# Start order, one moved statistic and new mixer delays in a two-layer decoder trunk on one Trainium2 core

## Chip, cores and metric

One Trainium2 chip, one core used. The metric is the device time of the program in microseconds; before the change the median of three runs is 1355.22 us (1355.17 to 1356.07).

## What is computed

Two layers over x of 256 tokens by 1024 features, float32. Each layer runs three sub-layers, each with a norm before and one after:

```
for i in range(DEPTH):                                   # 2 layers
    f = swiglu_ffn(rmsnorm(x, pre), w_in, w_out)         # 1024 -> 2*2816 -> 1024
    x = x + 0.5 * rmsnorm(f, post)
    p = rmsnorm(x, mpre) @ mix_w_in                      # q, k, v, z, beta, a, glu, gates
    y_a = gated_deltanet(...)                            # conv4+silu on q,k,v; chunked delta rule; norm; w_o
    y_b = conformer_conv(...)                            # a*sigmoid(g); 31-tap causal conv; layernorm; silu; w_o
    x = x + rmsnorm((g_a * y_a + g_b * y_b) @ mix_w_out, mpost)
    f = swiglu_ffn(rmsnorm(x, pre2), w_in2, w_out2)
    x = x + 0.5 * rmsnorm(f, post2)
```

## The kernel before

Tokens stand in two blocks of 128 (`tb` 0 and 1). All weights are streamed from HBM once, in pieces of 128 by 1024 (512 KB), some of 128 by 544. `Stream.load_one` issues a piece's transfer on SP's queue into `raw` (four buffers), ScalarE casts it into `whi` (the high part), and VectorE or GpSimd subtracts to get `wlo` (the low part). Activations are split in the same way into `xt` high and low. Every product is then three matmuls (`mm3`): high by high, high by low, low by high. In the profile such a matmul is `mm<-whi,xt` or `mm<-wlo,xt`.

A program order is written out for TensorE (`manual_schedule`). Products of a projection run in the order of the pieces, and after each pair of k tiles `lanes.tick()` is called. `Lanes` holds side jobs, generators that issue a few instructions at each step (transposes, convolutions, the delta rule, casts). A job's step comes due a number of ticks after the one before it, and that number stands in the table `DELAY`; `PLAN` gives the order of the mixer's column chunks and which jobs each one starts; `AFTER` and `LATE` say which jobs must be over, and by how many ticks, before one starts; the 31-tap convolution (`c0` to `c3`, accumulators `cacc`) and the inverse (`inv`, tile `iu`) have no due time and fill VectorE and GpSimd. In `Stream` a piece's cast and subtraction come due `lag` and `lag2` ticks after its load. ScalarE, VectorE and GpSimd then run in the order that the scheduler makes of all this, with the priorities in `CFG`; every engine executes its list in order.

The places that the prediction speaks of:

- **The start** (`start`, `half`, lines 470 to 525 of the kernel): seven matmuls on zeros (`idle`), then x is transposed in groups of four 128 by 128 tiles (`tr<-cst,x`; the identity `cst` and the scale `first_w` come on ScalarE's queue). ScalarE writes the four high parts `xt`, VectorE the four low parts. SP's first issues are: x of block 0 in two halves, the first weight piece, all of x of block 1, four more pieces. The first chunk of the first FFN takes its four pieces one after another, both token blocks for each. A job `first` does block 1's two transposed halves, then the two sums of squares (`jk`).
- **The end of each sub-layer** (`post`): for a token block, ScalarE squares and sums the two 512-column accumulators (`jk`), VectorE scales them into `fw`, adds up the sums (`ss`), GpSimd takes the power (`rpost`), VectorE adds to x. It runs twelve times; only the last one has no products beside it.
- **From FFN1 to the mixer** (`pre`, jobs `pre0` and `pre1`): the new x is normed into `xw`, transposed in halves, and split into `xt` while the last products of the FFN and the first of the mixer run.
- **The middle of the mixer**: VectorE does the short convolutions `c`, the decay products `at`, the 31-tap convolution and most `wlo`, each of them in its turn.

Of the kernel before, what the change touches and what calls it, by code (L numbers as in the profile page):

```python
# [9 lines left out]
F32 = mybir.dt.float32  # L10
# [5 lines left out]
P = 128  # L16
# [29 lines left out]
    "first": (1, 2), "ffn": (3, 5, 12), "pre0": (13, 7, 8, 4, 3, 3), "pre1": (15, 16, 0, 13, 8),  # L46
    "yt0": (10, 0, 10, 10, 26), "yt1": (10, 2, 0, 3, 3), "f_g0": (5, 0, 2, 1), "f_g1": (5, 1, 1, 1), "c0": (0, 0),
    "f_k1": (0, 1, 3, 1, 1, 3), "f_ka": (2, 0, 3), "decays": (12, 4, 2, 15, 4), "dts": (51, 3, 0, 0, 19, 19),
# [197 lines left out]
class Stream:  # L246
# [16 lines left out]
    def load_one(self, parts=1):  # L263
# [5 lines left out]
        nc.sync.dma_start(raw[:, :n], src)  # L269
# [54 lines left out]
def trunk(ctx: ExitStack, tc: tile.TileContext, x_in, wfirst, consts, feat, pch, tokp,  # L324
# [62 lines left out]
    for hf in range(2):  # L387
        nc.sync.dma_start(x[0][:, hf * 512:hf * 512 + 512], x_in[0:P, hf * 512:hf * 512 + 512])
        if hf == 0:
            nc.scalar.dma_start(cst[:, 0:P], consts[:, 0:P])  # L390
            nc.scalar.dma_start(first_w, wfirst)
# [87 lines left out]
    def start():  # L479
        r = [small(1, f"rstd{tb}") for tb in range(2)]  # L480
        xh = [halves(tb) for tb in range(2)]

        def half(tb, hf):
            tr = ps_tr()
            for k in range(4):
                T.transpose(tr[:, k, :], x[tb][:, (hf * 4 + k) * P:(hf * 4 + k + 1) * P], ident)
            t = xh[tb][hf]
            for k in range(4):
                S.activation(t[:, 0, k, :], tr[:, k, :], AF.Copy, scale=first_w[:, hf * 4 + k:hf * 4 + k + 1])
            for k in range(4):  # L490
# [971 lines left out]
```

## Time and profile before

| | us |
|---|---|
| median of three runs | 1355.22 |
| the profiled execution | 1356.38 |
| its span, from the first to the last instruction | 1354.4 |
| around the span | 1.98 |

The profile belongs to an execution of its own, 1.16 us above the median of the runs. TensorE is busy in 98% of the span, VectorE in 68%, ScalarE in 54%, GpSimd in 33%. With TensorE this full, read where it is *not* busy, or runs slowly, and follow what ended each of those times.

### The profile page before, as it was taken

The page shows a single profiled execution, that of the slowest core. Times are in us where ns is not written, and L with a number is a line of the kernel's source. Part 1 is how long each engine was busy: PE and PEld are TensorE (multiplying, and loading weights), DVE is VectorE, ACT ScalarE, POOL GpSimd, SP SyncE. Part 2 cuts the span into 40 slices and gives each one's busy share as a digit, 9 for nine tenths or more (in the row PEclk, how much of TensorE's full clock was granted, in tenths as well). Part 3 has the DMA queues.
Part 4 walks back from the last instruction along what each step waited for, and adds up shares of the span by engine and source line. Part 5 has one row for each costly group of instructions (what it writes and reads, how often), then busy time and mean ns, then how long its engine had stood idle before and what let it go on. Part 6 is the DMA issues. An engine that isn't in the chain of part 4 may idle for free.

```text
span 1354.4 us, 20203 instructions
## 1 busy us (share of the span) xinstructions
PE 1331.3 (98%) x7259; PEld 1132.3 (84%) x7259; DVE 926.9 (68%) x1593; ACT 730.8 (54%) x1172; POOL 446.4 (33%) x372
## 2 busy tenths in 40 slices
PE   9999999998999999999999999999989999999998
PEld 7888878997888888888888888799978878888886
DVE  6666456999966676765476654579999566766553
ACT  6554447666555545554455553577555564555541
POOL 0111025798834201111001110278986432011110
PEclk9999999999999999999999999999999999999999
DMA  7877745553634666876478775464545446477760
GB/s 273 284 259 248 232 164 192 185 191 114 196 125 147 212 229 207 281 253 218 148 230 278 263 236 186 143 233 172 172 143 166 151 139 233 157 258 254 257 225 33
DMA packets 114644, 273.76 MB, mean 202 GB/s; under 512 B 24656, under 2 KB 47728, under 8 KB 114544
## 3 DMA queue, kind: packets, MB, share of 16 engines
q1 hardware_dynamic: 114256, 272.40, 60.1%
q8 instruction: 57, 0.93, 0.3%
q14 instruction: 43, 0.35, 0.1%
q10 hardware_dynamic: 288, 0.07, 0.0%
HBM read 256.68 MB, written 15.75 MB: 201 GB/s over the span
## 4 chain that ended last, share of the span: by engine, by line
PE 81%; DVE 9%; POOL 3%; ACT 3%; issue 2%; DMA 1%; DVEq 0%; POOLq 0%; ACTq 0%
PE mm L143 75%; PE gd L143 4%; DVE cacc L123 3%; DVE c L123 3%; PE tr L149 2%; POOL wlo L123 2%; DVE wlo L123 2%; DMA raw<-mw 1%; ACT whi L170 1%; POOL rk L123 1%; DVE at L123 1%; ACT dt L170 1%; PE gd L149 0%; ACT sg L170 0%; ACT cf L170 0%
## 5 line engine op out<-in xcount | busy, mean ns | idle before, releaser
L143 PE MATMUL mm<-whi,xt 128*128 128x512 f32 (+1 forms) x2048 | 648.4, 392 | 4.8 <-ACT qT L170 2.3
L170 ACT CAST whi<-raw 128x1024 fp32r<-128x1024 f32 (+2 forms) x445 | 459.4, 1041 | 321.6 <-PE mm L143 201.4
L123 DVE TENSOR_TENSOR wlo<-raw,whi 128x1024 fp32r<-128x1024 f32 (+1 forms) x341 | 425.0, 1258 | 199.3 <-ACT whi L170 193.5
L143 PEld LDWEIGHTS mm<-whi,xt 128*128 128x128 f32 x2048 | 383.2, 188 | 85.2 <-DVE xt L123 4.9
L143 PE MATMUL mm<-wlo,xt 128*128 128x512 f32 (+1 forms) x1024 | 396.7, 387 | 0.5 <-DVE wlo L123 0.5
L123 POOL TENSOR_TENSOR wlo<-raw,whi 128x1024 fp32r<-128x1024 f32 (+1 forms) x104 | 247.4, 2394 | 142.5 <-ACT whi L170 138.1
L143 PEld LDWEIGHTS mm<-wlo,xt 128*128 128x128 f32 x1024 | 193.1, 189 | 37.2 <-DVE wlo L123 1.0
L143 PE MATMUL mm<-whi,act 128*128 128x512 f32 x704 | 218.3, 390 | 0.0
L123 POOL TENSOR_TENSOR act<-way,act 128x512 fp32r<-128x512 f32 x44 | 78.6, 1785 | 406.1 <-ACT act L170 396.4
L123 DVE SCALAR_TENSOR_TENSOR cacc<-hT,pc,cacc 128x254 f32<-128x254 f32 (+28 forms) x464 | 179.5, 470 | 0.2
L143 PE MATMUL mm<-xt,whi 128*128 128x256 f32 x960 | 175.0, 284 | 0.5 <-ACT qT L170 0.5
L143 PEld LDWEIGHTS mm<-whi,act 128*128 128x128 f32 x704 | 132.2, 188 | 27.5
L143 PEld LDWEIGHTS mm<-xt,whi 128*128 128x128 f32 x960 | 149.5, 192 | 1.2 <-ACT qT L170 0.8
L143 PE MATMUL mm<-wlo,act 128*128 128x512 f32 x352 | 137.0, 389 | 0.0
L143 PE MATMUL mm<-xt,wlo 128*128 128x256 f32 x480 | 135.8, 283 | 0.0
L143 PEld LDWEIGHTS mm<-xt,wlo 128*128 128x128 f32 x480 | 92.0, 192 | 0.0
L170 ACT ACTIVATE ag<-mm,rstd 128x256 f32<-128x256 f32 x88 | 41.8, 475 | 91.3 <-PE mm L143 75.2
L123 DVE SCALAR_TENSOR_TENSOR ag<-mm,rstd,ag 128x256 f32<-128x256 f32 x88 | 42.4, 481 | 54.0 <-ACT ag L170 53.8
L143 PEld LDWEIGHTS mm<-wlo,act 128*128 128x128 f32 x352 | 66.1, 188 | 13.5
L123 POOL TENSOR_TENSOR rpost<-ss,exp 128x1 f32<-128x1 f32 x12 | 6.5, 538 | 194.1 <-DVE ss L123 194.1
L123 DVE SCALAR_TENSOR_TENSOR fw<-mm,wbc 128x512 f32<-128x512 f32 x24 | 16.5, 687 | 46.4 <-ACT jk L170 46.4
L170 ACT ACTIVATE jk<-mm 128x512 f32<-128x512 f32 x24 | 14.4, 598 | 62.3 <-PE mm L143 62.3
(187 smaller groups left out, 1180.7 us busy)
## 6 DMA issues: line engine op xcount, KB each, us to landing
raw<-mw SPq DMA_DIRECT2D x168, 512.0 KB, 3.7
raw<-w1i SPq DMA_DIRECT2D x88, 512.0 KB, 4.7
raw<-w2i SPq DMA_DIRECT2D x88, 512.0 KB, 4.8
raw<-w1o SPq DMA_DIRECT2D x44, 512.0 KB, 4.3
raw<-w2o SPq DMA_DIRECT2D x44, 512.0 KB, 4.2
way<-way SPq DMA_DIRECT2D x176, 64.0 KB, 1.8
way<-way SPq DMA_DIRECT2D x44, 256.0 KB, 4.8
wbc<-feat SPq DMA_DIRECT2D x13, 512.0 KB, 4.5
```

Of the source, the lines that this page charges most:

```text
L123: r = op(out, *a, **k)
L143: r = self.eng.matmul(o, w, x, **k)
L149: r = self.eng.transpose(*a)
L170: r = op(*a, **k)
```

## The change

Five edits. (1) x and the first two pieces are loaded in parts and in the order of use, with the first transposes two at a time (`turn`), and each of the two first pieces is cast and subtracted in two halves, with the casts placed by hand. (2) In the first chunk (`lead`) pieces are taken two at a time for each token block. (3) In `post` the sum `ss` and the power are issued ahead of the second `fw`. (4) The tables `PLAN`, `DELAY`, `LATE`, `POOL` and some numbers of `CFG` are new. (5) The second part of `cst` and the first `wbc` are loaded later.

```diff
 PLAN = [
...
-    ("q0", ["f", "qt0"]), ("q1", ["f", "qt1", "qs", "cn"]), ("v0", ["f", "vt0"]), ("z0", ["s1", "s0"]),
+    ("q0", ["f", "qt0"]), ("q1", ["f", "qt1", "qs", "cn", "s1"]), ("v0", ["f", "vt0"]), ("z0", ["s0"]),
...
 DELAY = {
-    "first": (1, 2), "ffn": (3, 5, 12), "pre0": (13, 7, 8, 4, 3, 3), "pre1": (15, 16, 0, 13, 8),
+    "first": (1, 1, 4, 4, 3, 2, 2), "ffn": (20, 5, 36), "pre0": (13, 0, 8, 4, 0, 0),
+    "pre1": (15, 40, 10, 13, 8, 8, 8), "yt0": (10, 0, 10, 10, 26, 23, 26, 26), "yt1": (10, 0, 3, 3, 3, 3),
...
-LATE = {"inv": 20, "cn": 12, "sim0": 6, "sim1": 6, "merge": 7, "dts": 14}
+LATE = {"inv": 21, "cn": 15, "sim0": 6, "sim1": 7, "merge": 11, "dts": 10}
...
@@ load_one
-        nc.sync.dma_start(raw[:, :n], src)
+        for k in range(parts):
+            c = slice(k * n // parts, (k + 1) * n // parts)
+            r = nc.sync.dma_start(raw[:, c], src[:, c])
+            self.last = getattr(r, "ins", r)
...
+        if parts > 1:
+            yield
         for k in range(parts):
-            if k:
-                yield
             c = slice(k * n // parts, (k + 1) * n // parts)
             high(c)
+            if parts > 1:
+                yield
             low(c, self.gp if self.side[i] else self.vec)
+            if parts > 1:
+                yield
@@ start
+        def turn(tb, ks):
+            tr = ps_tr()
+            for i, k in enumerate(ks):
+                T.transpose(tr[:, i, :], x[tb][:, k * P:(k + 1) * P], ident)
...
         piece = st.load_one(2)
-        half(0, 0)
         next(piece)
-        nc.sync.dma_start(x[1], x_in[P:2 * P, :])
-        half(0, 1)
+        nc.sync.dma_start(x[0][:, 2 * P:4 * P], x_in[0:P, 2 * P:4 * P])
+        second = st.load_one(2)
+        next(second)
+        nc.sync.dma_start(x[1][:, 0:4 * P], x_in[P:2 * P, 0:4 * P])
+        nc.sync.dma_start(x[0][:, 4 * P:], x_in[0:P, 4 * P:])
+        pair = turn(0, (0, 1))
+        next(piece)
+        next(pair)
+        next(piece)
+        next(pair, None)
+        next(piece)
         next(piece, None)
 
         def steps():
+            for _ in turn(0, (2, 3)):
+                pass
+            for _ in second:
+                pass
+            yield
             half(1, 0)
+            st.load()
+            nc.sync.dma_start(x[1][:, 4 * P:], x_in[P:2 * P, 4 * P:])
+            yield
+            half(0, 1)
             st.load()
             yield
             half(1, 1)
@@ post
+        r = small(1, "rpost")
         for hf in range(2):
             cs = slice(hf * 512, hf * 512 + 512)
             S.activation(jk[:, cs], acc[hf], AF.Square, scale=D ** -0.5, accum_out=ss[:, hf:hf + 1])
+            if hf:
+                rms_scale(r, ss[:, 0:1], ss[:, 1:2])
             V.scalar_tensor_tensor(fw[:, cs], acc[hf], half, wbc[:, cs], op0=ALU.mult, op1=ALU.mult)
-        r = small(1, "rpost")
-        rms_scale(r, ss[:, 0:1], ss[:, 1:2])
@@ proj_in
-            for i in range(8 // chunks[c][1]):
+            b = 2 if lead and c == 0 else 1
+            for i in range(0, 8 // chunks[c][1], b):
                 for tb in range(c < first, 2):
-                    piece(c, tb, i, ps[tb], st.peek(0))
-                st.done()
+                    for j in range(b):
+                        piece(c, tb, i + j, ps[tb], st.peek(j))
+                for j in range(b):
+                    st.done()
```

Three places show what the engines' lists became.

**ScalarE at the start.** Its casts of weights (`whi`) and the high parts of x (`xt`), before:

```order
L170 ACTIVATE xt<-tr,first_w 128x128 x4
L170 CAST whi<-raw 128x512
L170 ACTIVATE xt<-tr,first_w 128x128 x4
L170 CAST whi<-raw 128x512
L170 ACTIVATE xt<-tr,first_w 128x128 x4
L170 CAST whi<-raw 128x1024
L170 ACTIVATE xt<-tr,first_w 128x128 x4
L170 CAST whi<-raw 128x1024 x2
L170 ACTIVATE jk,ss<-x_74 128x1024
```

and now:

```order
L171 CAST whi<-raw 128x512
L171 ACTIVATE xt<-tr,first_w 128x128 x2
L171 CAST whi<-raw 128x512
L171 ACTIVATE xt<-tr,first_w 128x128 x2
L171 CAST whi<-raw 128x512 x2
L171 ACTIVATE xt<-tr,first_w 128x128 x4
L171 CAST whi<-raw 128x1024
L171 ACTIVATE xt<-tr,first_w 128x128 x4
L171 CAST whi<-raw 128x1024 x3
L171 ACTIVATE xt<-tr,first_w 128x128 x4
L171 CAST whi<-raw 128x1024
L171 ACTIVATE jk,ss<-x_74 128x1024
```

The first cast stands ahead of the first two `xt`; three casts of 1024 columns, two of them of the second chunk's pieces, now stand ahead of the last four `xt`, where one stood. VectorE's list follows the same pattern with `wlo`. On TensorE the transposes that those last four need stood behind 12 products of the first chunk's 48 and now stand behind 30; the first product stood behind eight transposes and now stands behind two.

**VectorE from FFN1 to the mixer**, before:

```order
L123 SCALAR_TENSOR_TENSOR fw<-mm,wbc 128x512
L123 TENSOR_TENSOR wlo<-raw,whi 128x1024
L123 TENSOR_TENSOR xt<-tr,xt 128x512
L123 TENSOR_TENSOR wlo<-raw,whi 128x1024
L123 TENSOR_TENSOR xt<-tr,xt 128x512
L123 SCALAR_TENSOR_TENSOR fw<-mm,wbc 128x512
```

and now:

```order
L124 SCALAR_TENSOR_TENSOR fw<-mm,wbc 128x512
L124 TENSOR_TENSOR wlo<-raw,whi 128x1024
L124 TENSOR_TENSOR xt<-tr,xt 128x512 x2
L124 TENSOR_TENSOR wlo<-raw,whi 128x1024
L124 TENSOR_SCALAR ss_1693<-ss_1693 128x1
L124 SCALAR_TENSOR_TENSOR fw<-mm,wbc 128x512
```

The second low part of x stands ahead of the second `wlo`, no longer behind it, and `ss` ahead of `fw`.

**VectorE in the middle of the mixer**, around the first decay products `at`, before:

```order
L123 SCALAR_TENSOR_TENSOR cacc<-hT_1696,pc,cacc 128x251 x2
L123 SCALAR_TENSOR_TENSOR cacc<-hT_1696,pc,cacc 128x250 x2
L123 SCALAR_TENSOR_TENSOR cacc<-hT_1696,pc,cacc 128x249 x2
L123 SCALAR_TENSOR_TENSOR at<-gd,sc,dt 128x128 x8
L123 SCALAR_TENSOR_TENSOR cacc<-hT_1696,pc,cacc 128x248 x2
```

and now:

```order
L124 SCALAR_TENSOR_TENSOR cacc<-hT_1722,pc,cacc 128x251 x2
L124 SCALAR_TENSOR_TENSOR cacc<-hT_1722,pc,cacc 128x250 x2
L124 SCALAR_TENSOR_TENSOR at<-gd,sc,dt 128x128 x4
L124 SCALAR_TENSOR_TENSOR cacc<-hT_1722,pc,cacc 128x249 x2
L124 SCALAR_TENSOR_TENSOR at<-gd,sc,dt 128x128 x4
L124 SCALAR_TENSOR_TENSOR cacc<-hT_1722,pc,cacc 128x248 x2
```

The pair `cacc` of 249 columns moved from ahead of the first `at` to behind it. From the first `at` to the last convolution `c` ahead of the transposes of v, VectorE's list now has 60 `cacc` of the 31 taps where it had 58; the 16 `at`, the 6 `wlo` of 1024 columns and the rest are the same in number. Ahead of that stretch a `wlo` of 544 columns is new in the list, which GpSimd did before.

## Rows read from the trace of the kernel before

**Rows 1.** The page: busy time of each engine; the chain that ended last, by engine.
```profile
PE 1331.3 (98%) x7259; PEld 1132.3 (84%) x7259; DVE 926.9 (68%) x1593; ACT 730.8 (54%) x1172; POOL 446.4 (33%) x372
PE 81%; DVE 9%; POOL 3%; ACT 3%; issue 2%; DMA 1%; DVEq 0%; POOLq 0%; ACTq 0%
```
**Rows 2.** Busy time of a stretch inside an FFN stage: from and to, length, then busy time and number of instructions of each engine, TensorE's clock, DMA share, GB/s.
```profile
30.00:90.00 60.00, 60.00 (x266) 49.71 (x265) 39.81 (x49) 32.22 (x42) 9.25 (x5) 1.00 0.83 269
```
**Rows 3.** The chain at the start in order of time: start, length, what.
```profile
9.57 0.85 PE tr L149 x4
10.42 2.56 PE mm L143 x6
12.98 0.85 PE tr L149 x4
13.84 10.22 PE mm L143 x44
```
**Rows 4.** The timeline of the start, all engines: start, length, engine, line, operation, in brackets idle time before it and what ended it.
```profile
4.29 1.91 PE L149 MATMUL tr<-cst,x 128*128 128x128 f32 x8
5.39 1.14 ACT L170 ACTIVATE xt<-tr,first_w 128x128 fp32r<-128x128 f32 x4 [2.73 <-PE tr L149]
6.41 0.63 ACT L170 CAST whi<-raw 128x512 fp32r<-128x512 f32 x1
7.09 0.80 PE L143 MATMUL mm<-whi,xt 128*128 128x512 f32 x1 [0.89 <-ACT whi L170]
8.35 0.80 PE L143 MATMUL mm<-wlo,xt 128*128 128x512 f32 x1 [0.46 <-DVE wlo L123]
11.48 1.06 ACT L170 CAST whi<-raw 128x1024 fp32r<-128x1024 f32 x1
12.68 1.21 DVE L123 TENSOR_TENSOR wlo<-raw,whi 128x1024 fp32r<-128x1024 f32 x1
```
**Rows 5.** Transfers of the first six microseconds: what, queue, number, size, median us from issue to landing.
```profile
x<-x SPq DMA_DIRECT2D x2, 256.0 KB, 3.4
```
**Rows 6.** The timeline from FFN1 to the mixer, layer 0: TensorE's holes and what VectorE did.
```profile
191.52 1.22 DVE L123 TENSOR_TENSOR wlo<-raw,whi 128x1024 fp32r<-128x1024 f32 x1
193.39 0.73 PE L143 MATMUL mm<-whi,xt 128*128 128x512 f32 x2 [0.43 <-DVE xt L123]
194.80 1.27 DVE L123 TENSOR_TENSOR wlo<-raw,whi 128x1024 fp32r<-128x1024 f32 x1 [1.46 <-ACT whi L170]
195.99 0.68 DVE L123 TENSOR_TENSOR xt<-tr,xt 128x512 fp32r<-128x512 f32 x1
196.00 0.39 PE L143 MATMUL mm<-wlo,xt 128*128 128x512 f32 x1
196.72 0.74 PE L143 MATMUL mm<-whi,xt 128*128 128x512 f32 x2 [0.34 <-DVE xt L123]
203.69 0.39 PE L143 MATMUL mm<-whi,xt 128*128 128x512 f32 x1
204.12 0.63 PE L149 MATMUL tr<-cst,xw 128*128 128x128 f32 x4
```
**Rows 7.** The same place in layer 1.
```profile
864.27 0.39 PE L143 MATMUL mm<-wlo,xt 128*128 128x512 f32 x1
864.98 0.73 PE L143 MATMUL mm<-whi,xt 128*128 128x512 f32 x2 [0.32 <-DVE xt L123]
```
**Rows 8.** Busy time by stretch in the middle of the mixer of layer 0 (columns as in rows 2).
```profile
280.00:300.00 20.00, 20.00 (x169) 20.00 (x168) 20.00 (x58) 13.34 (x21) 19.89 (x11) 1.00 0.58 166
320.00:340.00 20.00, 16.38 (x87) 13.04 (x86) 19.97 (x45) 11.63 (x27) 17.96 (x30) 1.00 0.29 107
```
**Rows 9.** The timeline there: VectorE around the first `at`, and TensorE's hole at the transposes of v.
```profile
275.05 0.48 DVE L123 SCALAR_TENSOR_TENSOR hT<-mm,pc,sg 128x256 f32<-128x256 f32 x1 [0.63 <-ACT sg L170]
281.38 5.42 DVE L123 SCALAR_TENSOR_TENSOR cacc<-hT,pc,cacc 128x248 f32<-128x248 f32 x14
333.49 1.15 PE L149 MATMUL tr<-cst,vT 128*128 128x128 f32 x6 [1.45 <-ACT vT L170]
336.70 2.05 PE L143 MATMUL gd<-qT,kT 128*128 128x128 f32 x16
```
**Rows 10.** The same place in layer 1: the last products of the block in the timeline, and a stretch with TensorE's clock (third number from the end).
```profile
1004.56 3.38 PE L143 MATMUL gd<-qT,kT 128*128 128x128 f32 x16
1004.00:1006.00 2.00, 2.00 (x10) 1.81 (x9) 2.00 (x6) 1.36 (x4) 1.76 (x5) 0.50 0.00 0
```
**Rows 11.** Two small operations of GpSimd in the timeline, and what VectorE ran beside the second.
```profile
313.94 0.42 POOL L123 TENSOR_TENSOR iu<-iu,ia 128x133 f32<-128x133 f32 x1
314.44 1.42 POOL L123 TENSOR_TENSOR iu<-iu 128x133 f32<-128x133 f32 x1
314.34 1.22 DVE L123 TENSOR_TENSOR wlo<-raw,whi 128x1024 fp32r<-128x1024 f32 x1
```
**Rows 12.** The timeline of the end.
```profile
1348.43 0.69 DVE L123 SCALAR_TENSOR_TENSOR fw<-mm,wbc 128x512 f32<-128x512 f32 x1 [2.03 <-ACT jk L170]
1349.04 0.20 DVE L123 TENSOR_SCALAR ss<-ss 128x1 f32<-128x1 f32 x1
1349.38 0.54 POOL L123 TENSOR_TENSOR rpost<-ss,exp 128x1 f32<-128x1 f32 x1 [10.34 <-DVE ss L123]
1349.96 1.42 DVE L123 SCALAR_TENSOR_TENSOR x<-fw,rpost,x 128x512 f32<-128x512 f32 x2 [0.72 <-POOL rpost L123]
```

More of the change, by code (lines that the diff above doesn't have):

```diff
@@ L45 @@
 DELAY = {
-    "first": (1, 2), "ffn": (3, 5, 12), "pre0": (13, 7, 8, 4, 3, 3), "pre1": (15, 16, 0, 13, 8),
-    "yt0": (10, 0, 10, 10, 26), "yt1": (10, 2, 0, 3, 3), "f_g0": (5, 0, 2, 1), "f_g1": (5, 1, 1, 1), "c0": (0, 0),
-    "f_k1": (0, 1, 3, 1, 1, 3), "f_ka": (2, 0, 3), "decays": (12, 4, 2, 15, 4), "dts": (51, 3, 0, 0, 19, 19),
[2 rows of a table removed]
+    "first": (1, 1, 4, 4, 3, 2, 2), "ffn": (20, 5, 36), "pre0": (13, 0, 8, 4, 0, 0),
+    "pre1": (15, 40, 10, 13, 8, 8, 8), "yt0": (10, 0, 10, 10, 26, 23, 26, 26), "yt1": (10, 0, 3, 3, 3, 3),
+    "f_g0": (5, 0, 2, 1), "f_g1": (7, 1, 1, 1, 1), "c0": (0, 0), "f_k1": (0, 1, 3, 1, 1, 3), "f_ka": (2, 0, 3, 19),
+    "decays": (12, 4, 2, 15, 4), "dts": (51, 2, 0, 0, 19, 14), "kt1": (17, 3, 12, 1, 4),
[2 rows of a table added]
     "f_g3": (0, 1, 3, 1, 1, 1, 1), "f_v0": (0, 0, 1, 1, 0, 0, 0), "vt0": (20, 0, 0, 28, 0, 37, 6, 0),
[2 rows of a table removed]
[2 rows of a table added]
     "qt1": (0, 10, 28, 21, 20, 0, 17, 14), "f_q1": (1, 1, 3, 1, 1, 0), "qs": (0, 28, 31, 24, 19),
[2 rows of a table removed]
[2 rows of a table added]
 }
@@ L70 @@
 FILL = (("c3", "c2", "c1", "c0"), ("inv",))
-LATE = {"inv": 20, "cn": 12, "sim0": 6, "sim1": 6, "merge": 7, "dts": 14}
-POOL = {5, 7, 8, 11, 13, 16, *range(18, 21), 23, *range(29, 33), 35, 36, *range(39, 45), *range(47, 50), 51, 53, 55, 58, 60, 61, 63, 65, 67, 68, *range(70, 73), 77, 78, 84, 85}
-CFG = dict(stat=500, conv=50, ev=300, tok=4, st=4, post=-800, pre=1000, fin=None, turn=None, tokens=-100, glu=100, dec=200, dts=-100, kt=-400, vt=1000, qt=50, inv=1000, sim=100, merge=-400, scan=50, norm=200, onorm=-100, yt=-400, w=50, tails=4, ahead=1.5, lag=6, free=3, aheadp=3, lag2=3, bias=2, held=1)
+LATE = {"inv": 21, "cn": 15, "sim0": 6, "sim1": 7, "merge": 11, "dts": 10}
+POOL = {5, 7, 8, 12, 13, 16, *range(18, 21), 23, *range(29, 34), 35, 36, *range(39, 45), *range(46, 49), 51, 53, 55, 58, 59, 61, 63, 65, 67, 68, 70, 72, 77, 78, 84, 85}
+CFG = dict(stat=500, conv=50, ev=300, tok=4, st=4, post=-800, pre=1000, fin=None, turn=100, tokens=-100, glu=100, dec=200, dts=-100, kt=0, vt=1000, qt=-400, inv=1000, sim=-400, merge=-400, scan=50, norm=0, onorm=-100, yt=-400, w=50, tails=4, ahead=1.5, lag=10, free=3, aheadp=3, lag2=3, bias=2, held=1)
 KIND = {"f_g0": "glu", "f_g1": "glu", "f_g2": "glu", "f_g3": "glu", "decays": "dec", "dts": "dts", "kt0": "kt", "kt1": "kt",
@@ L386, in trunk @@
         T.matmul(warm_ps, idle[:, 0:P], idle[:, P:640], start=True, stop=True)
[L387 to L391, printed above, removed]
+    nc.sync.dma_start(x[0][:, 0:2 * P], x_in[0:P, 0:2 * P])
+    nc.scalar.dma_start(cst[:, 0:P], consts[:, 0:P])
+    nc.scalar.dma_start(first_w, wfirst)
     ident = cst[:, K_ID:K_ID + P]
@@ L481, in start @@
         xh = [halves(tb) for tb in range(2)]
-        def half(tb, hf):
[L484 to L490, printed above, removed]
-                V.scalar_tensor_tensor(t[:, 1, k, :], tr[:, k, :], first_w[:, hf * 4 + k:hf * 4 + k + 1],
-                                       t.bitcast(F32)[:, 0, k, :], op0=ALU.mult, op1=ALU.subtract)
+        def turn(tb, ks):
+            tr = ps_tr()
+            for i, k in enumerate(ks):
+                T.transpose(tr[:, i, :], x[tb][:, k * P:(k + 1) * P], ident)
+            for i, k in enumerate(ks):
+                S.activation(xh[tb][k // 4][:, 0, k % 4, :], tr[:, i, :], AF.Copy, scale=first_w[:, k:k + 1])
+                if i % 2:
+                    yield
+            for i, k in enumerate(ks):
+                t = xh[tb][k // 4]
+                V.scalar_tensor_tensor(t[:, 1, k % 4, :], tr[:, i, :], first_w[:, k:k + 1], t.bitcast(F32)[:, 0, k % 4, :],
+                                       op0=ALU.mult, op1=ALU.subtract)
+        def half(tb, hf):
+            for _ in turn(tb, range(4 * hf, 4 * hf + 4)):
+                pass
         def stat(tb):
@@ L502, in start @@
         piece = st.load_one(2)
-        half(0, 0)
         next(piece)
-        nc.sync.dma_start(x[1], x_in[P:2 * P, :])
-        half(0, 1)
+        nc.sync.dma_start(x[0][:, 2 * P:4 * P], x_in[0:P, 2 * P:4 * P])
[9 more added lines that the diff above has]
+        next(piece)
         next(piece, None)
         def steps():
+            for _ in turn(0, (2, 3)):
+                pass
+            for _ in second:
+                pass
+            yield
             half(1, 0)
+            st.load()
+            nc.sync.dma_start(x[1][:, 4 * P:], x_in[P:2 * P, 4 * P:])
+            yield
+            half(0, 1)
             st.load()
@@ L546, in mm3, with proj_in @@
         T.matmul(o, xl, wh, start=False, stop=stop)
-    def proj_in(xt, chunks, ev, fin, first=2, by_ch=(), xj=None):
+    def proj_in(xt, chunks, ev, fin, first=2, by_ch=(), xj=None, lead=False):
         def piece(c, tb, i, ps, w):
@@ L683, in fin @@
             lanes.add("ffn", steps())
-        proj_in(xt, [(512, 2)] * 11, ev, fin, first)
+        proj_in(xt, [(512, 2)] * 11, ev, fin, first, lead=not first)
         wbc = load_feat(l, wpost, 17)
```

12 rows, old and new, of the table DELAY are left out of this document.

## Prediction, made before the changed kernel ran

> **What bounds the kernel now.** I read the page first, then a stretch inside a stage, then the places where TensorE waits, in order of time. The page gives TensorE 98% of the span, and the chain that ended last runs through TensorE for 81% [rows 1]. Inside an FFN stage it is busy 60.00 of 60 us [rows 2]: a change to the order of casts, loads or statistics there moves nothing, as long as no cover breaks. What can be won lies in the holes between TensorE's instructions and at its low clock. They are in five places: the start [rows 3, 4], FFN1 to mixer [rows 6, 7], the middle of the mixer [rows 8, 9], a slow stretch in layer 1 [rows 10], and the end [rows 12]. The stage matters more than the average: VectorE is busy 68% of the span, but 20.00 and 19.97 of 20 us in the mixer's middle [rows 1, 8]. There it is the bound, and TensorE drops to 16.38 of 20.
>
> **The end (edit 3).** The last `post` now issues `ss` and the power ahead of the second `fw`. Today `fw` begins at 1348.43, `ss` follows at 1349.04, the power takes 0.54 from 1349.38, and x starts at 1349.96 [rows 12]. With `ss` first, all of that moves up by the 0.61 us between `fw` and `ss`, and `fw` (0.69) runs beside the power, between `ss` and x. Term: **-0.6**. In the other eleven uses products cover it. What could take it back is a slower power beside VectorE. Beside a VectorE `wlo` a small operation of GpSimd took 1.42 us, while its neighbour in time took 0.42 [rows 11]: 1.0 more, which would turn -0.6 into +0.4. The page "GPSIMD Engine Reference" of the Trainium skill, section "8. Key points", says that GpSimd shares its SBUF interfaces with VectorE and contends with VectorE instructions that have two SBUF inputs; the trace agrees for `wlo`, whose two inputs are both in SBUF, and by that rule `fw` would not contend, since one of its inputs is an accumulator. I keep -0.6, with ends -0.7 and +0.4, since the power's 0.54 is nearer to the 0.42 row than to the other.
>
> **FFN1 to mixer (edits 3, 4).** In layer 0 the low part of x's second half waits in VectorE's list behind a `wlo` (194.80, 1.27 us, itself late since its cast was late), so it starts only at 195.99 and TensorE, with a product issued at 196.00, issues the next at 196.72 instead of 0.23 later: 0.49 us lost, and about 0.1 more on the slower restart (0.73 for the next two products) [rows 6]. The new order has both low parts behind the first `wlo`, so this hole goes. The chain through block 1's `post` also gains the 0.6 of edit 3, which closes the 0.20 between 203.69 and 204.12 [rows 6]. The first hole, which ended at 193.39 on a low part behind the `wlo` of 191.52, stays: that `wlo` still stands ahead. Layer 1 shows the second hole with 0.71 from product to product, 0.48 lost [rows 7], so again some 0.6 with its restart, and little at the end. Sum 0.8 and 0.7: **-1.5**, with ends -2.0 (if half of the first holes goes too) and -0.4 (if the transposes, now ahead of six products more, wait for the second `xw`).
>
> **The start (edits 1, 2, 5).** Bytes and arithmetic are the same, in three transfers more on SP; the order is new. Today eight transposes run from 4.29, ScalarE writes four `xt` (1.14), then casts (0.63), and the first product starts at 7.09 [rows 4]. Now the first weight half is second in SP's queue, where the second half of x stood, 256 KB like it: issued behind one transfer, at about 1.2, and by 3.4 from issue to landing [rows 5] there near 4.6. A cast (0.63) and two `xt` (2 x 0.29) put the first product at 5.6 to 6.0, 1.3 earlier. The second product stands at 8.35, 1.26 behind the first, where 0.427 would do [rows 3, 4]: 0.83 more, which goes too, since its `wlo` is now made ahead of x's low parts. From 8.35 on the chain shows no break up to 13.84 and after [rows 3]. So 2.1 us are to be had, less some 0.7 for holes that the smaller groups of transposes leave: 1.4. But that is time at the low clock: six products took 2.56 us, 0.427 each, forty-four later ones 10.22, 0.232 each [rows 3]; the first is the 1.2 GHz level, the second 2.4. So 1.4 us are 3.3 products, worth 0.8 us later on.
>
> Against this stands a new hole. The last four `xt` now stand behind three casts of 1.06 on ScalarE [rows 4], where one stood, and their low parts behind `wlo` of 1.21 on VectorE. Two casts and two subtractions too many are 2.1 and 2.4 us, side by side; between the transposes and the products that need them TensorE has six products (1.4 us at 0.232) to cover them, and part of that goes to the `xt` themselves (1.14): a hole of 1.0 to 1.7 us late in the first chunk. I take 1.4, so that without the clock the start loses 0.6.
>
> The clock decides. TensorE's 0.427 spacing lasted to the last transposes before 13.84, 5.5 us after the chain became unbroken at 8.35. Now it is unbroken from about 6 to 7. If the level changes earlier by as much, 1.4 to 2.4 us, or by somewhat more, each microsecond saves 0.46 (0.195 of every 0.427); I take 2.2 us, 1.0. Term: 0.6 - 1.0 = **-0.4**, with ends -1.4 (4.4 us earlier) and +1.2 (no earlier, and the hole at 2.0). The page "TensorE: Matmul & The Clock Gate" of the Trainium skill, section "What's actually happening", says that the number of slow matmuls at a start varies between runs of one kernel; by that no gain from the clock could be counted on, and the start would stand at +0.6. One trace cannot show it.
>
> **The mixer (edit 4).** In the middle VectorE has no idle time [rows 8], so what it must do before the transposes of v decides. The pair of `cacc` that moved behind the first `at` is 2 x 0.39 (5.42 for 14), **+0.77** for v in each layer; in exchange the `at` come earlier, by at most that pair less the 544-column `wlo` that VectorE takes over (about half of 1.22), where 0.63 of idle time [rows 9] can also be filled. I put the `at` 0.45 earlier, so v is 0.3 later, and the hole that ends at 333.49 (1.45 idle) grows by that; nothing covers it, as the products ahead are used up. Other moved steps (state and merges 3 to 12 products earlier, kT's transposes later) lie under products; a step on SP or GpSimd's queues adds nothing there. Per layer +0.3, less some closing of smaller holes: **+0.3** for both, with ends -3.0 (each layer's 1.45 wholly gone) and +3.1 (0.77 whole, and 0.8 of the holes behind it, in each).
>
> **Sum.** -0.6 - 1.5 - 0.4 + 0.3 = -2.2. Against the profiled execution (1356.38 with 1.98 around its span) that is 1354.2; it stood 1.16 above the median, which the slow stretch of layer 1 (below) can explain whole. Against the median, 1355.22: **1353.0**.
>
> **Rivals.**
> - *The start loses.* The clock level changes no earlier and the casts of the second chunk hold back the last `xt`: +1.2 for -0.4, so 1355.22 - 0.6 - 1.5 + 1.2 + 0.3 = 1354.6. For it: three casts in a row in ScalarE's list. Against: TensorE has fewer holes to keep the clock down. That the orders change only what products cover, and the end alone remains, gives 1354.6 as well.
> - *The holes in the mixer close.* Then its +0.3 is -2.0, and with the start at its better end, -1.4: 1355.22 - 0.6 - 1.5 - 1.4 - 2.0 = 1349.7. For it: most of the table was rewritten, and TensorE's 16.38 of 20 [rows 8] is where the room is. Against: the block that waits for v keeps its place among the products.
> - *Slower: v's wait brings the low clock into both layers.* In layer 1 the sixteen `gd` took 3.38 us at a granted clock of 0.50, in layer 0 2.05 at full clock [rows 9, 10]: 1.33 us, after the same holes. If v comes 0.77 later and the holes after it grow by 0.8 in each layer, the idle time ahead of the `gd` is longer, and layer 0 falls as well. Price 3.1 + 1.33 = 4.4, less 2.5 from the other places: +1.9, 1357.1; with the start's loss too, 1358.7. It decides from the point at which layer 0's idle time ahead of the `gd` is longer than layer 1's is now.
>
> **How the numbers follow.** A measurement of this kernel tells about 0.2%, 2.7 us, from no change, so the bound on the fast side is 1352.5. My case has 0.45, between 1351.4 and 1354.0; 0.19 of it lies below 1352.5. The start's loss has 0.20, all but 0.01 within 0.2%. The mixer's closing, 0.25, is faster by over 0.2%. The slower case has 0.10, of which 0.06 lies above 1357.9. So faster 0.44, same 0.49, slower 0.07. The range from 1349.6 to 1355.6 leaves out the slower case, the half of the second rival that goes beyond its price, and thin ends: together 0.2.
>
> **What would show it.** The end: `ss` ahead of the second `fw`, a power of 0.54, and x some 0.6 sooner after the last product. FFN1 to mixer: in each layer one hole on `xt` left, not two. The start: a first product at 6 or before, the spacing near 0.23 by 12, and a hole on the last `xt` or their low parts late in the first chunk. The mixer: VectorE full as before, and the transposes of v waiting 1.5 to 2 us. I am wrong if v's wait is gone or doubled, if the level at the start changes near 14 again, or if a hole appears inside an FFN stage.

## The result: 0.2% slower

The changed kernel took 1358.03 us (median of 16 runs, 1354.89 to 1362.31); the kernel before, run beside it, 1355.05. The ratio is 1.0021, interval 1.0011 to 1.0030: some 3 us slower, where 2.2 less were forecast. The profiled execution took 1356.31 (span 1354.4), by chance the span of before's profile, though it lies 1.7 us below its own median and before's 1.3 above: the two traces show where time went, and the runs how much. The page:

```profile
PE 1332.0 (98%) x7259; PEld 1132.9 (84%) x7259; DVE 918.7 (68%) x1596; ACT 737.4 (54%) x1173; POOL 426.7 (32%) x370
```

Against [rows 1] nothing moved: a change of 0.2% is not read from the page. The view of waits, for TensorE (waited for, us in all, times, longest), shows it; after:

```profile
PE tr L150 <- ACT vT L171: 3.7, 3, 1.4
PE tr L150 <- DMA x<-x: 2.9, 1, 2.9
PE mm L144 <- ACT qT L171: 1.5, 2, 1.0
PE tr L150 <- ACT vr L171: 1.4, 2, 0.7
PE mm L144 <- DVE xt L124: 0.7, 1, 0.7
```

and the same view of the kernel before:

```profile
PE tr L149 <- ACT vT L170: 2.9, 2, 1.5
PE mm L143 <- ACT qT L170: 2.8, 4, 1.1
PE tr L149 <- ACT sq L170: 1.7, 2, 0.8
PE mm L143 <- DVE xt L123: 1.6, 4, 0.5
```

The four waits on `xt` from FFN1 to the mixer are gone (the 0.7 stands at the start), one of 2.9 us for x is new, and the waits around v and q are shared out anew. (`cf`, in both views with 3.4, is left out.) What this view can't show is the clock: stretches with TensorE's granted clock in the third column from the end (the two places of [rows 9, 10]), before, then after:

```profile
330.00:342.00 12.00, 9.52 (x59) 7.70 (x58) 11.97 (x30) 5.77 (x16) 10.67 (x21) 1.00 0.11 40
1000.00:1012.00 12.00, 9.74 (x53) 8.49 (x54) 11.96 (x27) 5.42 (x15) 10.71 (x20) 0.86 0.24 65
```
```profile
330.00:342.00 12.00, 9.51 (x42) 8.15 (x43) 11.97 (x30) 5.58 (x16) 10.43 (x23) 0.72 0.15 45
1000.00:1012.00 12.00, 9.98 (x46) 8.61 (x46) 11.97 (x30) 5.36 (x14) 10.59 (x22) 0.72 0.14 45
```

TensorE is as busy but issues fewer products, at a clock that now falls in both layers: it is granted 0.50, the lower of two levels, for 3.4 us before (layer 1) and for 6.8 us in each layer after.

**The start** (timeline; compare [rows 4]):

```profile
5.40 0.61 PE L144 MATMUL mm<-whi,xt 128*128 128x512 f32 x1 [0.47 <-ACT xt L171]
5.86 0.50 PE L144 MATMUL mm<-wlo,xt 128*128 128x512 f32 x1
7.32 0.40 PE L144 MATMUL mm<-whi,xt 128*128 128x512 f32 x1
10.65 0.66 PE L150 MATMUL tr<-cst,x 128*128 128x128 f32 x4 [2.94 <-DMA x<-x]
```

The chain that ended last has one long piece there, the first line below: the first half of block 1's x. The view of transfers over the first 12 us gives a median of 7.2 us from issue to landing for the three pieces of x of 256 KB (both halves of block 1 and the second half of block 0); the two that came first before took 3.4 [rows 5].

```profile
3.53 7.08 DMA x<-x
```
```profile
x<-x SPq DMA_DIRECT2D x3, 256.0 KB, 7.2
```

Before, all of x of block 1 went in one transfer, which took less (same view) and was issued 1.4 us sooner, at 2.11:

```profile
x<-x SPq DMA_DIRECT2D x1, 512.0 KB, 5.7
```

**FFN1 to mixer** (VectorE, then TensorE; compare [rows 6]): both low parts run in one go, and one hole, of 0.30, is left (0.20 before).

```profile
192.31 1.28 DVE L124 TENSOR_TENSOR xt<-tr,xt 128x512 fp32r<-128x512 f32 x2
194.56 1.35 DVE L124 TENSOR_TENSOR wlo<-raw,whi 128x1024 fp32r<-128x1024 f32 x1 [0.97 <-ACT whi L171]
```
```profile
203.40 0.63 PE L150 MATMUL tr<-cst,xw 128*128 128x128 f32 x4 [0.30 <-DVE xw L124]
```

**The transposes of v** in layer 0, then the `gd` of layer 1 (timeline of TensorE; compare [rows 9, 10]). `gd` is the PSUM tile that takes the mixer's small products, here sixteen of q and k:

```profile
330.41 0.63 PE L150 MATMUL tr<-cst,vT 128*128 128x128 f32 x2 [1.05 <-ACT vT L171]
332.46 1.12 PE L150 MATMUL tr<-cst,vT 128*128 128x128 f32 x6 [1.42 <-ACT vT L171]
336.01 3.62 PE L144 MATMUL gd<-qT,kT 128*128 128x128 f32 x16
...
1004.95 3.62 PE L144 MATMUL gd<-qT,kT 128*128 128x128 f32 x16
```

The 16 `gd`, 2.05 us in layer 0 before, take 3.62 in both layers.

**The end** (timeline; compare [rows 12]): `ss` now stands ahead of the second `fw` and the power runs beside it, and x starts 2.08 us after the last product began. Before, the last product was this, and x came 2.68 behind it (1349.96):

```profile
1347.28 0.39 PE L143 MATMUL mm<-whi,act 128*128 128x512 f32 x1
```

After:

```profile
1348.00 0.39 PE L144 MATMUL mm<-whi,act 128*128 128x512 f32 x1
1349.15 0.21 DVE L124 TENSOR_SCALAR ss<-ss 128x1 f32<-128x1 f32 x1 [2.03 <-ACT jk L171]
1349.28 0.68 DVE L124 SCALAR_TENSOR_TENSOR fw<-mm,wbc 128x512 f32<-128x512 f32 x1
1349.50 0.54 POOL L124 TENSOR_TENSOR rpost<-ss,exp 128x1 f32<-128x1 f32 x1 [10.34 <-DVE ss L124]
1350.08 1.41 DVE L124 SCALAR_TENSOR_TENSOR x<-fw,rpost,x 128x512 f32<-128x512 f32 x2
```

### The profile page after: what moved, and what is told of

Read it like the earlier page. It is cut to its first block, busy times and chain, and to the rows that moved or that the text cites. A ratio compares the mean times of both kernels' runs of the same rounds, so it can differ in the third digit from the quotient of the medians.

```text
span 1354.4 us, 20218 instructions
## 1 busy us (share of the span) xinstructions
PE 1332.0 (98%) x7259; PEld 1132.9 (84%) x7259; DVE 918.7 (68%) x1596; ACT 737.4 (54%) x1173; POOL 426.7 (32%) x370
## 4 chain that ended last, share of the span: by engine, by line
PE 84%; DVE 5%; POOL 4%; ACT 3%; DMA 2%; issue 1%; SPq 0%; POOLq 0%; DVEq 0%; ACTq 0%
PE mm L144 77%; PE gd L144 4%; PE tr L150 2%; DVE cacc L124 2%; POOL iu L124 2%; ACT whi L171 1%; DMA raw<-mw 1%; POOL wlo L124 1%; DVE c L124 1%; DVE at L124 1%; ACT dt L171 1%; DMA x<-x 1%; DVE wlo L124 1%; DMA dA<-at 0%; ACT vr L171 0%
## 5 line engine op out<-in xcount | busy, mean ns | idle before, releaser
L124 DVE TENSOR_TENSOR wlo<-raw,whi 128x1024 fp32r<-128x1024 f32 (+2 forms) x344 | 420.3, 1229 | 276.1 <-ACT whi L171 270.8
L124 POOL TENSOR_TENSOR wlo<-raw,whi 128x1024 fp32r<-128x1024 f32 (+1 forms) x102 | 241.8, 2381 | 148.7 <-ACT whi L171 143.0
L124 POOL TENSOR_TENSOR act<-way,act 128x512 fp32r<-128x512 f32 x44 | 64.5, 1466 | 445.2 <-ACT act L171 445.2
L124 DVE SCALAR_TENSOR_TENSOR c<-mm,pc,c 128x255 f32<-128x255 f32 (+2 forms) x108 | 43.6, 473 | 0.0
```

What stands on the lines that cost most here:

```text
L124: r = op(out, *a, **k)
```

## The experiments

Every ratio is to the kernel before, run beside; in brackets its interval.

**One part alone.** e1 puts the new tables and the new `post` on the old start; e2 puts the new start and `post` on the old tables; e3 changes `post` alone; e4 is the changed kernel with x and the first pieces in large transfers.

```diff
 e3, against before
+        r = small(1, "rpost")
         for hf in range(2):
...
+            if hf:
+                rms_scale(r, ss[:, 0:1], ss[:, 1:2])
 e4, against the change
-        for k in range(parts):
...
+        nc.sync.dma_start(raw[:, :n], src)
...
-        nc.sync.dma_start(x[1][:, 0:4 * P], x_in[P:2 * P, 0:4 * P])
+        nc.sync.dma_start(x[1], x_in[P:2 * P, :])
```

> The change with the start of before (its loads, its transposes in fours, its casts): only the new tables and the moved statistic are left of it. Theory A (the start costs: x's later transfers land late, TensorE stands still for some 3 us in the first chunk, and its clock rises late in most executions): this kernel loses what the start cost and is at 1354.0 or below, 1 us or more under the kernel before. Theory B (the mixer costs: the low-clock stretch at the transposes of v is twice as long and comes in both layers): it stays at 1357 to 1358.5, like the change.

> The change with all tables of before (column plan, delays, lateness, engine choice, numbers): only the new start and the moved statistic are left. Theory A: 1358 to 1360, since the transitions' gain of the tables is gone and the start's loss stays; the profile shows a hole of 2 us or more before the transposes of x's second block. Theory B: 1354.0 to 1354.8, and the stretch at the transposes of v as in the kernel before.

> The kernel before with the moved statistic alone. Both theories: -0.6 us at the end, 1354.4, and nothing else; in the profile the power of the last sub-layer takes 0.54 beside fw. If GpSimd were slowed by VectorE there, 0.4 to 1 us more.

> The change with its first loads in large transfers again (x of block 0 in two halves, x of block 1 in one, the first two weight pieces whole, 256 to 512 KB each, in the order x0 first half, two pieces, x1, x0 second half) but with its order of transposes, casts and products. Theory A in the form that the small transfers are what makes the landings late: the first product comes later, near 7, but the hole before the transposes of x1 shrinks below 1 us and the kernel is at 1355 to 1356. Theory A in the form that the amount of data ahead of x1 makes it late (x1 stands behind 1.28 MB in either case): the hole stays. Theory B: within 1 us of the change, 1357 to 1359.

Measured: e1 1.0012 (1.0002 to 1.0022), e2 1.0045 (1.0029 to 1.0060), e3 0.9988 (0.9978 to 0.9997), e4 1.0014 (1.0003 to 1.0025). `post` is worth 1.6 us, more than the 0.6 at the end: it also closes one of the two holes on `xt` in each layer, as the waits of e3 show beside the 1.6 us in four of before:

```profile
PE mm L143 <- DVE xt L123: 0.9, 2, 0.5
```

Taken together, the rest of the change loses. e2 is worse than the whole change, which led to a count that the prediction had not made: `start` loads ten weight pieces ahead (2+1+1+1+1+3+1), the old one eight (1+1+1+1+3+1). Beside a kernel with nine (e5), VectorE's list in e2 has one `wlo` more ahead of the transposes of v.

**The pieces ahead, and the low clock.** e5 is e2 with one piece fewer (its text says eight; by the count above it is nine). e6 and e7 keep TensorE occupied with products of zeros at the transposes of v and q. e8 is e3 with the two rows `pre0` and `pre1` of the new table.

```diff
 e5, against e2
-            st.load(3)
+            st.load(2)
 e6, against the change (e7: 14 of 256 columns and 4 of 512, on e3)
+        def busy(t, count, k):
+            for _ in range(count):
+                nc.tensor.matmul(t.rearrange("p k c -> p (k c)"), idle[:, 0:P], idle[:, P:P + k * P], start=True, stop=True)
...
+                if gp == 0 and tb == 0:
+                    busy(tr, 5, 4)
...
+                    if gp == 0 and tb == 0 and hl == 2:
+                        busy(tr[:, 2:4], 12, 2)
 e8, against e3
-    "pre0": (13, 7, 8, 4, 3, 3), "pre1": (15, 16, 0, 13, 8),
+    "pre0": (13, 0, 8, 4, 0, 0), "pre1": (15, 40, 10, 13, 8, 8, 8),
```

> The new start and the moved statistic with all tables of before, as in e2_start_and_post, but with one load less at the end of the start, so that the stream of weights runs eight pieces ahead as before and not nine; VectorE's list in the middle of the mixer is then that of before. Theory C (the ninth piece puts one more wlo on VectorE ahead of the transposes of v, and the holes and the low clock there make most of e2's loss): 1353.5 to 1356, 5 us or more under e2, and no low-clock stretch over 3.5 us in the profile. Theory A (the start itself): it stays within 2 us of e2, 1359 to 1361.

> The change with products on zeros that nobody reads put into TensorE's list in the first layers' holes at the transposes of v and q (5 of 512 columns, 12 of 256, 4 of 512: some 3.2 us at 2.4 GHz, once in each layer). Theory B (the clock falls because TensorE idles there, and the low clock costs more than the wait): the low-clock stretches at 333 and 1002 us are gone from the profile and the kernel is 3 to 6 us faster than the change, 1352 to 1355. If the low clock has another cause, the products only add work: 1358 or above, and the stretches stay.

> The kernel before with the moved statistic, and the same products on zeros in the holes at v and q (14 of 256 columns, 4 of 512, some 2.3 us in each layer). Theory B: the low-clock stretch of layer 1 (3.41 us in e3's profile) goes, 0 to 2 us faster than e3, 1351.5 to 1353. If the filled products delay the transposes instead: 1354 or above.

> The kernel before with the moved statistic and the new delays of the jobs pre0 and pre1 alone (from FFN1 to the mixer); the rest of the tables is of before. By the prediction's term the second hole on xt goes in both layers: 1.0 to 1.4 us under e3, 1351.7 to 1352.2. If the holes there only move on to the mixer, whose VectorE is full, it is within 0.4 us of e3.

Measured: e5 1.0009 (1.0000 to 1.0019), e6 1.0011 (1.0002 to 1.0020), e7 0.9984 (0.9976 to 0.9993), e8 0.9975 (0.9967 to 0.9984). One piece less ahead gives back 4.9 us with the old tables. The zeros lift the clock; e6 in the two stretches:

```profile
330.00:342.00 12.00, 11.13 (x75) 9.36 (x76) 11.97 (x29) 5.72 (x15) 10.71 (x20) 1.00 0.15 46
1000.00:1012.00 12.00, 11.06 (x70) 9.18 (x69) 11.96 (x30) 5.11 (x14) 10.75 (x20) 1.00 0.15 49
```

That is worth 1.4 us of the change's 2.8 (1.0021 to 1.0011; the intervals overlap), not the 2 x 3.4 that two stretches of 6.8 us at half speed would suggest. VectorE stays full (11.97 of 12), and TensorE waits later instead, for ScalarE's `sq`: its waits in e6 have one on `gd`, of which the profile of the change itself has none. There TensorE comes from its slow stretch and reaches this place only at 355.90, in e6 at 354.40.

```profile
PE gd L150 <- ACT sq L171: 2.9, 2, 1.8
```

The two rows of e8 give 1.8 us more than `post` alone, beside the forecast's second term of 1.5.

**Which half of the tables.** f1 puts the other rows of `PLAN` and `DELAY` on e8, f2 `LATE`, `POOL` and `CFG`. f3 is e5 with whole transfers, f4 is e8 with four products of zeros in the old start's holes.

```diff
 f1, against e8 (three of the changed rows)
-    "sim1": (10, 0, 3, 6, 6, 14, 11, 8), "f_kb": (0, 0, 8), "kt0": (4, 1, 4, 0, 4),
-    "sim0": (23, 3, 8, 0, 0, 0, 3, 4), "inv": (75, 4, 9, 0, 14, 11, 4, 1), "f_g2": (0, 1, 1, 1), "c1": (7, 0),
+    "sim1": (20, 0, 2, 0, 6, 16, 16, 0), "f_kb": (0, 0, 5, 0), "kt0": (1, 0, 4, 0, 4, 4),
+    "sim0": (4, 3, 8, 0, 0, 22, 24, 4), "inv": (75, 6, 9, 0, 14, 11, 4, 1), "f_g2": (0, 1, 0, 1), "c1": (6, 3, 4),
 f2, against e8
-LATE = {"inv": 20, "cn": 12, "sim0": 6, "sim1": 6, "merge": 7, "dts": 14}
+LATE = {"inv": 21, "cn": 15, "sim0": 6, "sim1": 7, "merge": 11, "dts": 10}
...
 f4, against e8
+        if once:
+            busy()
```

> e8_post_transition (1351.5) with the new PLAN and the new DELAY of the mixer's and the FFN's jobs as well, but with LATE, POOL and CFG of before. Theory D (the jobs' new due times move the decay products, the transposes of kT and the state behind what VectorE must do before v, so the holes there grow): most of the tables' cost of 5 us, 1354.5 to 1357, with a low-clock stretch of 6.8 us in the profile. Theory E (the engine choice, lateness and priorities do it): 1351 to 1352.5.

> e8_post_transition with the new LATE, POOL and CFG, but with PLAN and DELAY of before. Theory D: 1351 to 1352.5. Theory E: 1354.5 to 1357. If neither part costs its share alone, the loss is in how the two meet.

> e5_start_eight_ahead (new start, moved statistic, tables of before, eight pieces ahead; 1356.5, 3.3 us over the same with the old start) with its first loads in large transfers again. If the small transfers make the start's loss: 1354.5 or below, no hole over 1 us before the transposes of x1. If it is the order of casts (the second chunk's two pieces ahead of the last four xt): within 1 us of e5, with the hole of 0.8 us near 18 to 19 us still there.

> e8_post_transition with two products on zeros ahead of the first product and two between the first and the second, in TensorE's idle times at the old start (0.9 and 0.8 us). If the date at which the clock rises at the start (5 to 14 us in the profiles so far) hangs on these idle times, it rises before 9 us, and the median falls by 0.5 to 2 us, to 1349.5 to 1351, with a smaller spread. If not, within 0.4 us of e8, or 0.3 slower.

Measured: f1 1.0073 (1.0059 to 1.0087), f2 1.0058 (1.0044 to 1.0072), f3 0.9996 (0.9986 to 1.0005), f4 0.9969 (0.9957 to 0.9981). Each half costs 11 to 13 us over e8, both together 4 or 5 (e1 or g1 less e8): the halves lean on each other, so neither can be charged alone. f4 is 4.2 us under before, but not set apart from e8 (the intervals overlap), nor f3 from e5. f1's largest hole, in TensorE's timeline, stands at 283.38 in layer 0 and again in layer 1:

```profile
283.38 2.07 PE L144 MATMUL gd<-kT 128*128 128x128 f32 x8 [3.48 <-DVE at L124]
```

**Start and tables apart.** g1 has the whole change but the old start, with ten pieces ahead; g4 has the new start and `post`, the old tables and eight. g2 is e1, g3 is f4, both with zeros at v and q as in e6 and e7.

```diff
 g1, against e1            g4, against e5
-            st.load(3)    -            st.load(2)
+            st.load(5)    +            st.load(1)
```

> The change with the start of before, but with ten pieces loaded ahead as the new start does: from the second chunk on every engine's list is that of the change. What it gains on the change (1358.0) is what the new start costs by itself. If the start costs 2 to 3 us whatever follows: 1355.0 to 1356.0. If the start costs nothing and the ten pieces and the tables make the whole loss: 1357.5 to 1358.5.

> e1_tables_and_post (new tables, moved statistic, old start, 1356.6) with products on zeros in TensorE's idle times at v and q (4 of 512 columns, 12 of 256, 4 of 512 in each layer). Theory B: no low-clock stretch at 330 and 1000 us, and 2 to 3 us faster than e1, 1353.6 to 1354.6. The waits for VectorE stay, so it does not come down to e8 (1351.5).

> f4_start_filled (moved statistic, new pre0 and pre1, products on zeros at the start; 0.9969 of before) with products on zeros at v and q as in e7. Low-clock stretches of 3.4 us there go: up to 1 us under f4, ratio 0.996 to 0.997 of before. If the products at v only take the place of the wait: the same as f4.

> The new start and the moved statistic with all tables of before and eight pieces ahead, as before (e5 had nine): from the second chunk on VectorE's and GpSimd's lists are those of e3. Against e3 (0.9988 of before) it is what the new start costs by itself: if 2 to 3 us, the ratio is 1.0003 to 1.0010; if the ninth piece made most of e5's loss, 0.9988 to 0.9995.

Measured: g1 1.0007 (0.9998 to 1.0015), g2 1.0001 (0.9993 to 1.0010), g3 0.9971 (0.9959 to 0.9983), g4 1.0000 (0.9991 to 1.0009). So the loss splits, in us of 1355: `post` -1.6 (e3), `pre0` and `pre1` -1.8 (e8 less e3), the rest of the tables with ten ahead +4.3 (g1 less e8), the new start +1.9 (the change less g1; g4 less e3 says +1.6): +2.8, each term uncertain by 1 to 2. In the profiles of g1 and e8 the clock is low for the same 3.4 us, and the spans still differ by 3.5 (1354.8 and 1351.3). With the clock full in the mixer of both, g2 is still 4.1 above g3, or 3.3 once the 0.8 by which f4 lies under e8, for its filled start, is taken off: the tables cost waits as well as clock. The waits of TensorE that tell them apart, in g2, then in g3 (all listed waits are 13.8 and 10.2 us):

```profile
PE gd L150 <- ACT sq L171: 2.5, 2, 1.5
PE mm L144 <- ACT qT L171: 1.2, 2, 0.8
PE tr L150 <- ACT stg L171: 0.8, 1, 0.8
PE gd L144 <- ACT sq L171: 0.7, 1, 0.7
```
```profile
PE mm L143 <- ACT qT L170: 2.8, 4, 1.1
```

The first is a new wait, once in each layer, at the transposes of `u`: `u` is what the delta rule's inverse gives, it comes back from HBM in eight loads of 32 KB, and the merge transposes it into `gd`. `sq` are the squares of the transposed q. The kernel gives both the same three PSUM buffers (`tag="tr", bufs=3`), so `gd` has to wait until `sq` has been read out of one. On `gd` 3.2 us are added, 2.5 of them at `u`, and 1.6 fall away on `qT`. In g1 (TensorE, ScalarE, SyncE's queue):

```profile
355.00 0.44 PE L150 MATMUL gd<-cst,u 128*128 128x128 f32 x2 [1.67 <-ACT sq L171]
```
```profile
353.40 1.04 ACT L171 CAST whi<-raw 128x1024 fp32r<-128x1024 f32 x1 [2.43 <-DMA raw<-mw]
354.35 0.59 ACT L171 ACTIVATE sq<-tr 128x512 f32<-128x512 f32 x1
```
```profile
345.09 4.41 SPq L976 DMA_DIRECT2D u<-dU  x8
349.60 7.67 SPq L270 DMA_DIRECT2D raw<-mw  x5
```

Read from below: SyncE issues the eight loads of `u` in a row, the weight piece behind them comes late, its cast waits 2.43, `sq` stands behind the cast, and TensorE behind `sq`. In e8 weight pieces stand between the loads and TensorE does not wait there; but there it also has 12 products between the `gd` ahead and this transpose, and in g1 nine. The first transpose of `u` is at 355.42 before, 355.58 in e8 and 355.00 in g1: there TensorE is through with what stands ahead of it 1.7 us sooner than that, and waits.

**SyncE's queue alone.** h1 (on g2) and h2 (on the change) lower the priority of six of the eight loads, so that weight pieces stand between them. No other engine's list moves.

```diff
+                    with tc.high_priority(offset=-1000 if (gp, j) > (1, 1) or gp == 0 else 0):
-                    nc.sync.dma_start(U[gp][js, :, js], du[gp, :, j].rearrange("t s c -> s t c"))
+                        nc.sync.dma_start(U[gp][js, :, js], du[gp, :, j].rearrange("t s c -> s t c"))
```

> Edit: the kernel of g2 (new tables, old start, zero products in the three holes of the v block; 1.0001 of before), with the eight small loads of the inverse (u) no longer in one row on SyncE's queue: after the first two, weight pieces stand between them, as in the kernel before. All other engines' lists are unchanged. SyncE theory: in g2 the eight u loads take 4.55 us on SyncE from 345.04, the next weight piece is issued only at 349.69, ScalarE's cast waits for it, the statistic sq stands behind that cast, and TensorE waits 1.46 us at 355.07 and about 1 us in layer 1. With the pieces between, these holes go: 2.0 to 2.5 us less, ratio 0.9982 to 0.9986. Rival: VectorE is full there and sets the end of the stage, so what is won at 355 is waited for later, before the transposes of xhat: no change, ratio 1.000 to 1.001.

> Edit: the changed kernel itself, with weight pieces between the u loads on SyncE's queue, as in h1; all other engines' lists are the changed kernel's. SyncE theory: the profile of the changed kernel has its low clock just ahead of this place, which delays TensorE so that the late piece is partly covered; where the low clock is shorter the hole is open. So 0.5 to 2 us less than the change's 1358.0: ratio 1.0006 to 1.0017. Rival (VectorE sets the end): 1.0021 as the change.

Measured: h1 1.0060 (1.0047 to 1.0074), h2 1.0055 (1.0042 to 1.0067): 8.0 and 4.6 us more, where one theory forecast less time and the other no change. `sq` no longer ends the wait, `u` does, and later; h1's wait and its first place:

```profile
PE gd L150 <- DMA u<-dU: 6.8, 2, 3.8
```
```profile
356.07 0.63 PE L150 MATMUL gd<-cst,u 128*128 128x128 f32 x4 [2.99 <-DMA u<-dU]
```

So parting the row of eight is no cure: with the transposes of `u` where the tables put them, `u` is needed so early that its loads have to go first, and then the weight piece behind them is late, as in g1. My theory, that pieces between the loads take the wait away, falls. Its rival, that what is won here is waited for later, is not tested, since nothing was won here; h1 shows only that a wait at `u` does reach the end. Of h1's 8.0 us, 4.3 are the wait (6.8 for 2.5); its granted clock also falls behind each wait (0.55 below, and 0.59 from 1029 to 1032 us), where g2 has 1.00, so that the rest may be clock:

```profile
356.80:360.20 3.40, 3.40 (x11) 2.57 (x10) 3.40 (x9) 1.75 (x4) 2.74 (x3) 0.55 0.19 74
```

## Why the prediction was wrong, by its steps

- **The end, -0.6: right.** x starts 2.08 after the last product began; in [rows 12] `ss` came 0.61 behind `fw`, and now stands ahead of it. The power took 0.54 beside `fw`, as before, so the rule of the Trainium skill ("GPSIMD Engine Reference", section "8. Key points"), which names two SBUF inputs, held for an operation with one input in an accumulator. `post` as a whole gave 1.6 (0.4 to 3.0, e3), the rest of it in the next item.
- **FFN1 to mixer, -1.5: right in sign, too small.** All four holes on `xt` went, not one in each layer. The sum priced `post` at the end alone, with products covering its other eleven uses; by the medians e3 gives 1.0 more than the 0.6, and there one hole in each layer is gone already. `pre0` and `pre1` took the other, 1.8 by e8 less e3. So end and transition together gave 3.4 where 2.1 were forecast. A hole of 0.30 on `xw` stayed in layer 0, where the 0.20 was to close.
- **The start, -0.4: wrong, +1.9.** What was in the sum came as worked out: first product at 5.40, the second 0.46 behind, and late holes on the last low parts (0.30 and 0.81 us) of 1.1, where 1.4 was taken. One failing step is that x's transfers, "three transfers more on SP", got no term: the first half of block 1's x is issued behind six others and lands at 10.61, and TensorE, out of work at 7.7, waits 2.94 (0.78 to 2.03 in the profiles of e2, e5, h2, g4 and e6). With whole transfers e4 has no such hole, but its first product comes only at 7.01:

```profile
7.01 0.50 PE L144 MATMUL mm<-whi,xt 128*128 128x512 f32 x1 [1.37 <-ACT xt L171]
```

  so it gains 0.9, and f3 1.8 over e5, both within the intervals. The other failing step is the clock's gain of 1.0, taken as the new start's own. In this profile the clock did rise sooner, and by more than the 2.2 us taken: the product at 7.32 takes 0.40, where products before stayed 0.43 apart to 14 (the column of the granted clock reads 1.00 from 4 to 14 us in both, so here the level is read from the products). But the old start can have it too. The same product of the same start in before, and in e3:

```profile
8.94 0.63 PE L143 MATMUL mm<-whi,xt 128*128 128x512 f32 x1
```
```profile
8.69 0.39 PE L143 MATMUL mm<-whi,xt 128*128 128x512 f32 x1
```

  Before, e8 and g1 show the late date, e1 and e3 the early one. What the start comes to is seen where the first chunk ends, at its 48th product; in before, e3 and after:

```profile
22.54 0.61 PE L143 MATMUL mm<-whi,xt 128*128 128x512 f32 x2
20.87 0.62 PE L143 MATMUL mm<-whi,xt 128*128 128x512 f32 x2
22.79 0.62 PE L144 MATMUL mm<-whi,xt 128*128 128x512 f32 x2
```

  The clock's date alone makes 1.67 in the old start, and with the early date in both the new one ends 1.92 later (0.7 to 1.2 in the profiles of g4, e6, e2 and e5). e4 and f3 end it at 21.88 and 22.11, no sooner: without the hole for x, too, this start loses, and why is not shown. The page "TensorE: Matmul & The Clock Gate" of the Trainium skill, section "What's actually happening", says that the number of slow matmuls at a start varies between runs of one kernel, and these runs agree. With no gain from the clock the start stood at +0.6, 1.3 short of +1.9. (The last transposes of block 1 stood behind nine products before, not 12 as counted ahead of the prediction; they moved by 21.)
- **The mixer, +0.3: wrong, +4.3.** The failing step is the sentence that "other moved steps (state and merges 3 to 12 products earlier ...) lie under products; a step on SP or GpSimd's queues adds nothing there". The +4.3 is the rest of the tables with ten pieces ahead, wherever it acts; the runs place it in the mixer, in two parts. The clock falls in both layers, and e6 gives 1.4 of that back. And the merge begins with the transposes of `u`; three products sooner, they open a wait that before did not have (2.3 us in g1, 2.5 in g2, 2.9 in e6). The change's own profile does not show it: after the slow stretch TensorE gets there later (355.90, in g1 355.00 after a wait of 1.67). Only the 0.77 of `cacc` ahead of v was priced, and the two more pieces loaded ahead, whose `wlo` also fall to VectorE ahead of v, were not counted (one of them costs 4.9 with the old tables, e2 less e5; with the new tables ten ahead cost no more than eight, g1 beside e1).
- **The slower rival was the right mechanism, in part.** The low clock did come into layer 0, with `gd` at 3.62 for 2.05 us. Its price was put at 1.33 for layer 0's `gd`, behind waits of 3.1 at v; e6 puts the clock of both layers at 1.4, and the rest is waits, in g2 most of all at `u`. It had a chance of 0.10, because I asked of layer 0 only whether v came later, not whether `u` and q did. It is not in every execution: the profile of g1, with the same tables, has the full clock at this place of layer 0.

What stays open: which entries of the tables pull the transposes of `u` forward, and how much of the 3.3 without the low clock is theirs; f1 and f2 show only that halves can't be told apart. The lowest median is that of `post` with `pre0`, `pre1` and zeros in the start's holes (f4, 0.9969): 4.2 us less than before and 7 less than the change.

## What to carry over

Where an edit mixes an order written by hand with a table of delays, price every place at which an engine's work is pulled forward, and on every queue: what comes sooner by three products can wait for what comes no sooner. Count what is loaded ahead, since each piece more is work on the engine that is full in the stage behind. A first product that starts 1.7 us earlier is worth nothing if the transfers behind it land later: look at when the first chunk ends, not when it begins.

## What was not expected of the hardware

- Products of zeros in TensorE's holes raise the clock (0.72 to 1.00 in both stretches of e6) and cost nothing that can be measured: f4 0.9969 beside e8's 0.9975, e7 0.9984 beside e3's 0.9988, e6 1.0011 beside 1.0021, all within the intervals. In g2 four of 512 columns run in what was idle time:

```profile
328.81 1.04 PE L1031 MATMUL tr<-idle 128*128 128x512 bf16 x4
```

- The date at which the clock rises differs by 7 us between executions whose instructions are the same up to there, so a term taken from one trace of the start is uncertain by 1.7 us (22.54 in before, 20.87 in e3).
- In the changed start 256 KB of x took 7.08 us to land, issued behind six transfers of 128 to 256 KB; the whole 512 KB took 5.7 before.
